# Weight sums by an adding transfer, and the half-wide chunk by seven block products, in the feed-forward nets of a two-layer model

## The chip, the cores and the metric

One Trainium2 chip, one of its cores. The metric is device time of one execution in microseconds, the median of several runs; 1072.19 us before the change (1072.14 to 1073.27 in three runs).

## The reference

Two layers, each with a feed-forward net, a mixer (convolution, recurrence, pooling), cross attention and a second net, with a layer norm behind each. Only the four nets matter here. All is float32, 256 tokens, width 1024, inner width 2816.

```
def swiglu(x, w_gate, w_up, w_down):
    return (jax.nn.silu(x @ w_gate) * (x @ w_up)) @ w_down

h = layer_norm(ALPHA * h + 0.5 * swiglu(h, ffn1_gate[l], ffn1_up[l], ffn1_down[l]), ln_g[l, 0], ln_b[l, 0])
...
h = layer_norm(ALPHA * h + 0.5 * swiglu(h, ffn2_gate[l], ffn2_up[l], ffn2_down[l]), ln_g[l, 3], ln_b[l, 3])
```

## The kernel before

**Numbers.** Each float32 operand is split into a high part (a cast to fp32r by ScalarE, ACT) and a low part (the difference, by VectorE, DVE): `split`, lines 60 to 62. A product is three matmuls: high by high, high by low, low by high (`mm_rows`, line 128). A weight tile of 128 x 1024 numbers (512 KB) is loaded into one of six buffers `raw`, cast to `whi` and differenced to `wlo`, with eight buffers each. So a ninth split waits until the first one's matmuls are done.

**A net.** `ffn` (line 400) goes through the inner width in six chunks: five of 512 columns and one of 256. Up to chunk c's activations it computes x @ gate and x @ up for these columns; then the second half of chunk c - 2's and the first half of chunk c - 1's rows are multiplied by `down` (`both`, line 683). The products of gate and up go to four accumulators `acc`, those of down to four accumulators `dn` that hold the net's whole output. At the end, `tail` adds the last three pieces of `down`, output block by output block, and `finish` (line 303) makes the layer norm and transposes its result for what comes next.

**Three ways to compute a chunk.** `hidden` (line 525) makes 2 x 2 x 8 block products of three matmuls. `by_seven` (line 555) takes x in 2 x 2 blocks (two token blocks, two halves of the width) and gate and up together as 2 x 2 blocks of weights: w00 and w10 are the upper and lower half of gate's rows, w01 and w11 those of up's. Seven block products instead of eight give the four results, from sums and differences of blocks of x (`bx`, made once in a net) and sums of weight blocks. Of the seven products in the kernel before, four have a sum as their weights: w00 + w01, w00 + w11, w01 + w11, w00 + w10. `parts_of` makes each in place with two additions of 128 x 1024 on DVE (line 584), eight in a chunk. `last_hidden` (line 641) computes the half-wide chunk with weights as the stationary operand, so that its results come out transposed, without a deal.

Nets 2 to 4 take chunks 2 and 4 by seven products, the first net chunk 4 alone (line 666). Chunk 5 is the half-wide one, in all nets by `last_hidden`.

**After the products** of the wide chunks the results are combined (`put`, line 605), gated (`left`, line 628), and turned (`turn`, line 446): four transfers deal the gated values `sg` by partitions to `dealt`, DVE transposes them into a buffer `square`, and a split gives the activations `ah` and `al`. The buffers of the half results `half` and of `square` have one tag, "up", with two buffers, so each waits for the one before the last to be done.

**What sets the order.** The code is written in the order of the program; a scheduler then places each engine's instructions in a queue of its own, and each queue runs in order. SP issues nearly all transfers, in order as well; an issue waits until its buffer is free.

Of the kernel before, what the change touches and what calls it, by code (L numbers as in the profile page):

```python
# [8 lines left out]
F32 = mybir.dt.float32  # L9
# [3 lines left out]
ALU = mybir.AluOpType  # L13
# [4 lines left out]
P = 128  # L18
DEPTH = 2
SEQ = 256  # L20
DM = 1024
# [25 lines left out]
def model(ctx: ExitStack, tc: tile.TileContext, t: dict, out: bass.AP):  # L47
# [12 lines left out]
    def split(hi, lo, src):  # L60
        nc.scalar.copy(hi, src)  # L61
        lows.append(nc.vector.tensor_tensor(lo, src, hi.bitcast(F32), op=ALU.subtract))  # L62
# [45 lines left out]
    def sums(o):  # L108
        return o.rearrange("p (c h) -> p h c" if len(o.shape) == 2 else "p r (c h) -> p r h c", h=2)
# [24 lines left out]
    def tok(i):  # L134
        return slice(i * P, (i + 1) * P)
# [264 lines left out]
    def ffn(l, name, n, pend=None, last=False, early=None):  # L400
        gate, up, down = (t[f"{name}_{x}"][l] for x in ("gate", "up", "down"))
        with tc.tile_pool(name="ffn", bufs=2, reuse_waits="tile") as fp:
# [40 lines left out]

            def turn(s):
                ah, al = act_tiles()
                x = fp.tile([P, 4, NT, P], F32, tag="dealt", name="dealt", bufs=1)
                for a in range(4):
                    nc.sync.dma_start(x[a * 32 : a * 32 + 32], s[:, :, a * P : (a + 1) * P])  # L450
                for i in range(NT):
                    d = fp.tile([P, 4, P], F32, tag="up", name="square")
                    nc.vector.transpose(
                        d.rearrange("p k (b r) -> p b k r", b=4), x[:, :, i, :].rearrange("p b (k j) -> p b k j", k=4)
                    )
                    split(ah[:, :, tok(i)], al[:, :, tok(i)], d)
                return ah, al

            def first():
# [62 lines left out]
                        gated(s, i, ou)  # L522
                return turn(s)

            def hidden(c0, between=lambda: None):
                s = activations()
                o = all_products(load(gate, 0, NK, c0, CHUNK))
                for i in range(NT):
                    activate(s, i, o[i])
                between()  # L530
                o = all_products(load(up, 0, NK, c0, CHUNK))
                for i in range(NT):
                    gated(s, i, o[i])
                return turn(s)
# [17 lines left out]
                    split(*parts[n], q[o])  # L552
                return parts

            def by_seven(c0, bx):
                def rows_by_columns(r):
                    return r.rearrange("p (k c) -> p k c", c=CHUNK)

                def pieces(*tags):
                    return [  # L560
                        rows_by_columns(
                            (fp if "spare" in g else wp).tile([P, DM], F32, tag=g, name="raw", bufs=6 if g == "raw" else 1)
                        )
                        for g in tags
                    ]

                def block(m, j, to):
                    for i in range(2):
                        k = 4 * j + 2 * i
                        loads.append(nc.sync.dma_start(  # L570
                            to[i], m[k * P : (k + 2) * P, c0 : c0 + CHUNK].rearrange("(k p) c -> p k c", p=P)
                        ))
                    return to

                w00 = block(gate, 0, pieces("spare0", "spare1"))
                w01 = block(up, 0, pieces("lng", "lnb"))
                w11 = block(up, 1, pieces("raw", "raw"))
                w10 = block(gate, 1, pieces("spare2", "raw"))

                def parts_of(r, plus=None):  # L580
                    hi, lo = [], []
                    for i in range(2):
                        if plus is not None:
                            nc.vector.tensor_tensor(r[i], r[i], plus[i], op=ALU.add)  # L584
                        h = wp.tile([P, 1024], F32R, tag="whi", name="whi", bufs=8)
                        w = wp.tile([P, 1024], F32R, tag="wlo", name="wlo", bufs=8)
                        h, w = (rows_by_columns(x) for x in (h, w))
                        split(h, w, r[i])
                        hi.append(h)
                        lo.append(w)  # L590
                    return Weights(hi, lo, 2, [])

                def part_of_x(i, j):
                    d = slice(4 * j, 4 * j + 4)
                    return xTh[:, d, tok(i)], xTl[:, d, tok(i)]

                def run(o, x, w):
                    for k in range(4):
                        wh, wl = w.at(k, slice(0, CHUNK))
                        mm_rows(o, x[0][:, k, :], x[1][:, k, :], wh, wl, k == 0, k == 3)  # L600

                def half_sum():
                    return fp.tile([P, 4, P], F32, tag="up", name="half").rearrange("p k t -> p (k t)")

                def put(o, a, op, b):
                    nc.vector.tensor_tensor(halves(o), sums(a), halves(b), op=op)

                s = activations()
                g = [s[:, i, :] for i in range(NT)]
                o = [acc((P, CHUNK)) for _ in range(4)]  # L610
# [12 lines left out]
                run(o[0], bx[3], parts_of(w11))  # L623
                run(o[1], part_of_x(0, 1), parts_of(w10))
                run(o[2], part_of_x(1, 1), parts_of(w00, w10))


                def left():
                    put(e, o[0], ALU.add, e)
                    for i in range(NT):  # L630
                        put(g[i], o[1 + i], ALU.add, g[i])
                    s = fp.tile([P, NT, CHUNK], F32, tag="spare2", name="sg", bufs=1)
                    for i, u in enumerate((e, f)):
# [57 lines left out]
            def aside():  # L691

                with tc.issue_after(lows[-1].ins):
                    if bx:
                        rest[1]()
                    else:
                        bx.extend(blocks_of_x())

            for c, (c0, ncol) in enumerate(chunks):
                if not c:  # L700
                    acts.append(first())
                    ys = [[acc((P, 512), "dn") for _ in range(2)] for _ in range(NT)]
                elif c in sevens:
                    left = by_seven(c0, bx)
                else:
                    if c in (1, 2) and early is not None:
                        acts.append(hidden(c0, aside))
                    else:
                        acts.append(hidden(c0) if ncol == CHUNK else last_hidden(c0))
                if c == 1 and early is None:  # L710
                    bx.extend(blocks_of_x())
                if c == max(sevens) + 1:
# [495 lines left out]
```

## Time and profile before

| | |
|---|---|
| profiled execution, its own time | 1072.23 us |
| its span in the profile | 1070.2 us |
| median of three runs | 1072.19 us |
| granted TensorE clock, mean | 0.998 |
| DMA, mean | 217 GB/s |
| second net, from its chunk 2 to its end | 405 to 537 us of the span |

Times in the rows are microseconds from the start of the span, unless marked ns. PE is TensorE, DVE VectorE, ACT ScalarE, POOL GpSimd, SP the engine that issues transfers. In a row in order of time the first number is the start, the second the length of the merged piece (x5: five instructions). Instructions of one engine overlap by the end of their pipeline, so the pitch from one start to the next is shorter than the length of one: a 128 x 512 matmul lasts 0.38 us and the next starts after 0.216. In a row of a group stand its count, then the busy time, the mean ns of one, and the idle time of the engine just before them. A row of a transfer group ends with the KB of one and the median us from issue to landing.

### The profile page before, as it was taken

The numbers are of one execution on the slowest core, as the hardware profiler recorded it, in microseconds if no ns is written. First come the engines' busy times: TensorE is split into PE (matmuls) and PEld (weight loads), VectorE is DVE, ScalarE is ACT, GpSimd is POOL, SyncE is SP. The second block draws the span as 40 slices with busy tenths as digits, with TensorE's granted clock in tenths as the row PEclk, the third lists the DMA queues.
The fourth block names the chain that finished last, engine by engine and source line by source line (L and its number), as shares of the span: only waits on it lengthen the run. The fifth ranks groups of instructions, "written<-read, shape, count | busy, mean of one in ns | idle before, by whom it ended". The sixth has DMA issues, their size and how long they took to land.

```text
span 1070.2 us, 16314 instructions
## 1 busy us (share of the span) xinstructions
PE 1060.6 (99%) x5968; PEld 938.9 (88%) x5968; DVE 946.3 (88%) x1318; ACT 642.2 (60%) x916; POOL 65.0 (6%) x114
## 2 busy tenths in 40 slices
PE   9999999999999999999999999999999999999997
PEld 7888888889899888888888888888898998888886
DVE  6977997998998799999799999788989787999986
ACT  7556655767457565656575557566764665656660
POOL 9600001000000000000000000010000000000000
PEclk9999999999999999999999999999999999999999
DMA  9998395755575575948675875957536665759471
GB/s 360 259 298 269 119 281 167 251 188 159 177 271 168 181 247 198 292 167 226 236 260 192 250 261 173 298 168 227 190 128 208 247 230 176 259 151 341 133 220 40
DMA packets 130896, 231.90 MB, mean 217 GB/s; under 512 B 9409, under 2 KB 48609, under 8 KB 130817
## 3 DMA queue, kind: packets, MB, share of 16 engines
q1 hardware_dynamic: 129024, 228.49, 65.6%
q0 software_dynamic: 1216, 1.20, 0.5%
q8 instruction: 47, 0.77, 0.3%
q10 hardware_dynamic: 576, 1.18, 0.3%
q14 instruction: 33, 0.26, 0.1%
HBM read 216.15 MB, written 1.05 MB: 203 GB/s over the span
## 4 chain that ended last, share of the span: by engine, by line
PE 99%; DMA 0%; DVE 0%; issue 0%; DVEq 0%
PE acc L105 65%; PE dn L105 31%; PE acc L172 1%; PE dn L910 1%; DMA h<-in_x_dram 0%; PE dn L969 0%; PE dn L968 0%; PE dn L958 0%; PE acc L1034 0%; PE dn L472 0%; PE dn L875 0%; DVE h L358 0%; DVE h L353 0%; DVE st L338 0%; DVE h L326 0%
## 5 line engine op out<-in xcount | busy, mean ns | idle before, releaser
L61 ACT CAST whi<-raw 128x1024 fp32r<-128x1024 f32 (+1 forms) x438 | 442.4, 1042 | 199.3 <-DVE raw L584 54.7
L62 DVE TENSOR_TENSOR wlo<-raw,whi 128x1024 fp32r<-128x1024 f32 (+1 forms) x438 | 515.6, 1210 | 33.9 <-ACT whi L61 30.4
L105 PE MATMUL acc<-whi,xT 128*128 128x512 f32 x1032 | 312.9, 380 | 0.0
L105 PEld LDWEIGHTS acc<-whi,xT 128*128 128x128 f32 x1032 | 195.0, 189 | 27.5
L105 PE MATMUL acc<-wlo,xT 128*128 128x512 f32 x516 | 195.6, 379 | 0.0
L105 PE MATMUL acc<-xT,whi 128*128 128x512 f32 x576 | 142.2, 382 | 0.2
L105 PE MATMUL dn<-whi,ah 128*128 128x512 f32 x346 | 131.5, 380 | 0.0
L105 PE MATMUL dn<-wlo,ah 128*128 128x512 f32 x346 | 131.1, 379 | 0.0
L105 PE MATMUL dn<-whi,al 128*128 128x512 f32 x346 | 131.1, 379 | 0.0
L105 PEld LDWEIGHTS acc<-xT,whi 128*128 128x128 f32 x576 | 103.9, 190 | 12.5 <-ACT whi L61 0.7
L105 PEld LDWEIGHTS acc<-wlo,xT 128*128 128x128 f32 x516 | 97.5, 189 | 13.9
L105 PE MATMUL dn<-whi,xT 128*128 128x512 f32 x288 | 87.9, 381 | 0.0
L105 PEld LDWEIGHTS acc<-xT,wlo 128*128 128x128 f32 x576 | 75.5, 191 | 3.9
L105 PE MATMUL acc<-xT,wlo 128*128 128x256 f32 x576 | 75.9, 275 | 0.0
L105 PEld LDWEIGHTS dn<-wlo,ah 128*128 128x128 f32 x346 | 65.4, 189 | 9.2
L105 PEld LDWEIGHTS dn<-whi,al 128*128 128x128 f32 x346 | 65.4, 189 | 9.2
L105 PEld LDWEIGHTS dn<-whi,ah 128*128 128x128 f32 x346 | 65.4, 189 | 9.1
L584 DVE TENSOR_TENSOR raw<-raw 128x1024 f32<-128x1024 f32 x56 | 66.2, 1218 | 0.4
L350 POOL TENSOR_TENSOR rs<-rs,nhalf 128x1 f32<-128x1 f32 x16 | 14.9, 929 | 834.2 <-DVE rs L346 598.7
L105 PEld LDWEIGHTS dn<-whi,xT 128*128 128x128 f32 x288 | 54.6, 190 | 7.4
L105 PE MATMUL dn<-wlo,xT 128*128 128x512 f32 x144 | 54.6, 379 | 0.0
L332 DVE SCALAR_TENSOR_TENSOR h<-h,dn 128x512 f32<-128x512 f32 x31 | 21.2, 683 | 31.6 <-PE dn L105 31.6
(232 smaller groups left out, 1278.7 us busy)
## 6 DMA issues: line engine op xcount, KB each, us to landing
raw<-in_ffn_up_dram SPq DMA_DIRECT2D x88, 512.0 KB, 5.3
raw<-in_ffn_down_dram SPq DMA_DIRECT2D x88, 512.0 KB, 6.9
raw<-in_ffn_gate_dram SPq DMA_DIRECT2D x84, 512.0 KB, 5.0
raw<-in_w_in_dram SPq DMA_DIRECT2D x48, 512.0 KB, 4.7
dealt<-sg SPq DMA_DIRECT2D x80, 128.0 KB, 4.7
raw<-in_ca_k_dram SPq DMA_DIRECT2D x16, 512.0 KB, 5.1
raw<-in_w_out_dram SPq DMA_DIRECT2D x16, 512.0 KB, 4.3
raw<-in_ca_v_dram SPq DMA_DIRECT2D x16, 512.0 KB, 5.3
```

Source lines behind the costliest of these rows:

```text
L61: nc.scalar.copy(hi, src)
L62: lows.append(nc.vector.tensor_tensor(lo, src, hi.bitcast(F32), op=ALU.subtract))
L105: nc.tensor.matmul(o, w, x, start=start, stop=stop)
L172: nc.tensor.transpose(pt[:, k, :], src[:, (4 * j + k) * P : (4 * j + k + 1) * P], unit)
L332: nc.vector.scalar_tensor_tensor(v, v, ALPHA / scale, sums(y[i][n]), op0=ALU.mult, op1=ALU.add, accum_out=None if junk is None else st[:, ...
L350: nc.gpsimd.tensor_tensor(rs, rs, nhalf[:, 0:1], op=ALU.pow)
L584: nc.vector.tensor_tensor(r[i], r[i], plus[i], op=ALU.add)
L910: nc.tensor.matmul(o[g, hh, :], kc[:, hh, g], x, start=True, stop=True)
```

## The change

Four edits, all in `ffn`:

- The first and second block of up are summed by transfers (`sum_by_transfers`): SP loads w01 into the two buffers that else hold the layer norm's parameters, and GpSimd issues a second transfer of w11 with an addition at the destination. This is issued ahead of the up products of the chunk before.
- The seven products are other ones, in another order: first w00, w11 and w10 alone, then S = w00 + w01 + w11, w01 + w11, S - w11 = w00 + w01, and S + w10. With w01 + w11 there already, DVE makes three sums (or differences) of two operations each, six in a wide chunk.
- In nets 2 to 4 the half-wide chunk goes by seven products too, with 256 columns; there DVE also makes the sum w01 + w11. A block is one tile of 4 x 256, so a sum is one addition and a split one pair. The result is dealt and turned like that of a wide chunk.
- `between` holds what stood in `aside`, and issues the transfers.

```
-            sevens = (2, 4) if early is None else (4,)
+            sevens = (2, 4, 5) if early is None else (4,)
...
+            def sum_by_transfers(c0):
+
+                to = block(up, 0, c0, pieces("lng", "lnb"))
+                for i, r in enumerate(to):
+                    a = (4 + 2 * i) * P
+                    nc.gpsimd.dma_start(
+                        r, up[a : a + 2 * P, c0 : c0 + CHUNK].rearrange("(k p) c -> p k c", p=P), accum_op=ALU.add
+                    )
+                return to
...
-                run(o[0], part_of_x(0, 0), parts_of(w00))
-                nc.scalar.copy(halves(g[0]), sums(o[0]))
-                run(o[2], bx[0], parts_of(w00, w01))
-                run(o[1], bx[1], parts_of(w00, w11))
-                e = half_sum()
-                put(e, o[1], ALU.add, g[0])
-                run(o[3], bx[2], parts_of(w01, w11))
-                put(g[1], o[3], ALU.add, e)
-                f = half_sum()
-                put(f, o[2], ALU.subtract, g[1])
-                put(e, o[2], ALU.subtract, e)
-                o = [acc((P, CHUNK)) for _ in range(3)]
-                run(o[0], bx[3], parts_of(w11))
-                run(o[1], part_of_x(0, 1), parts_of(w10))
-                run(o[2], part_of_x(1, 1), parts_of(w00, w10))
+                if ncol < CHUNK:
+                    put(both_up, both_up, ALU.add, w11)
+                o = [acc((P, ncol)) for _ in range(4)]
+                run(o[0], part_of_x(0, 0), parts_of(w00))
+                e = half_sum()
+                nc.scalar.copy(halves(e), sums(o[0]))
+                run(o[1], bx[3], parts_of(w11))
+                f = half_sum()
+                nc.scalar.copy(halves(f), sums(o[1]))
+                run(o[2], part_of_x(0, 1), parts_of(w10))
+                combine(g[0], o[2], ALU.add, e)
+                put(w00, w00, ALU.add, both_up)
+                run(o[3], bx[1], parts_of(w00))
+                combine(e, o[3], ALU.add, e)
+                combine(f, f, ALU.subtract, e, apart=False)
+                o = [acc((P, ncol)) for _ in range(3)]
+                run(o[0], bx[2], parts_of(both_up))
+                combine(g[1], o[0], ALU.add, e)
+                put(both_up, w00, ALU.subtract, w11)
+                run(o[1], bx[0], parts_of(both_up))
+                put(w00, w00, ALU.add, w10)
+                run(o[2], part_of_x(1, 1), parts_of(w00))
...
                 def left():
-                    put(e, o[0], ALU.add, e)
-                    for i in range(NT):
-                        put(g[i], o[1 + i], ALU.add, g[i])
+                    combine(f, o[1], ALU.add, f)
+                    combine(e, o[1], ALU.subtract, g[1])
+                    combine(g[1], o[2], ALU.add, g[1])
...
-                    return turn(s)
+                    return turn(s, ncol // P)
...
+                if c + 1 in sevens:
+                    n = (c + 1) * CHUNK
+                    if n + CHUNK <= DFF:
+                        both_up[:] = sum_by_transfers(n)
...
-                    left = by_seven(c0, bx)
+                    left = by_seven(c0, bx, both_up if ncol == CHUNK else None)
```

Where the queues change. The numbers behind names tell buffers apart. First DVE in the second net, over the last products of chunk 2, before: `square` and `al` are chunk 1's activations, `wlo` low parts of weights, `L584` a weight sum, `half` and `sg` combines; `wlo_4460` belongs to the chunk's last product.

```order
L453 STREAM_TRANSPOSE square_4242<-dealt_4233 128x4x4x32
L62 TENSOR_TENSOR wlo_4434<-raw_4308,whi_4433 128x1024
L62 TENSOR_TENSOR al_4232<-square_4238,ah_4231 128x4x128
L62 TENSOR_TENSOR al_4232<-square_4242,ah_4231 128x4x128
L606 TENSOR_TENSOR half_4382<-acc_4314,sg_4312 128x512
L62 TENSOR_TENSOR wlo_4438<-raw_4309,whi_4437 128x1024
L62 TENSOR_TENSOR wlo_4455<-raw_4296,whi_4454 128x1024
L606 TENSOR_TENSOR sg_4312<-acc_4316,half_4382 128x512
L584 TENSOR_TENSOR raw_4297<-raw_4297,raw_4309 128x1024
L606 TENSOR_TENSOR half_4407<-acc_4315,sg_4312 128x512
L606 TENSOR_TENSOR half_4382<-acc_4315,half_4382 128x512
L62 TENSOR_TENSOR wlo_4460<-raw_4297,whi_4459 128x1024
```

The same place now: `raw` on the left is a weight sum (L596), L622 a combine, and `wlo_4458` and `wlo_4462` belong to the last product.

```order
L596 TENSOR_TENSOR raw_4155<-raw_4304,raw_4308 128x1024
L622 TENSOR_TENSOR sg_4315<-acc_4318,half_4340 128x512
L62 TENSOR_TENSOR wlo_4436<-raw_4154,whi_4435 128x1024
L622 TENSOR_TENSOR half_4340<-acc_4319,half_4340 128x512
L62 TENSOR_TENSOR wlo_4440<-raw_4155,whi_4439 128x1024
L622 TENSOR_TENSOR half_4362<-half_4362,half_4340 128x512
L622 TENSOR_TENSOR sg_4315<-acc_4409,half_4340 128x512
L596 TENSOR_TENSOR raw_4303<-raw_4303,raw_4311 128x1024
L596 TENSOR_TENSOR raw_4304<-raw_4304,raw_4312 128x1024
L622 TENSOR_TENSOR half_4362<-acc_4410,half_4362 128x512
L62 TENSOR_TENSOR wlo_4458<-raw_4303,whi_4457 128x1024
L62 TENSOR_TENSOR wlo_4462<-raw_4304,whi_4461 128x1024
```

The transposes have moved ahead of this piece, and three sums stand between the fifth product's splits and the last one's, where one stood.

Next DVE in the second net's chunk 5, before: the last three of the chunk's four splits of weights (5101 to 5152), then those of the slabs of `down` behind them.

```order
L62 TENSOR_TENSOR wlo_5101<-raw_5093,whi_5100 128x1024
L62 TENSOR_TENSOR wlo_5148<-raw_5143,whi_5147 128x1024
L62 TENSOR_TENSOR wlo_5152<-raw_5144,whi_5151 128x1024
L62 TENSOR_TENSOR wlo_5207<-raw_5202,whi_5206 128x1024
L62 TENSOR_TENSOR wlo_5211<-raw_5203,whi_5210 128x1024
L62 TENSOR_TENSOR wlo_5243<-raw_5238,whi_5242 128x1024
L453 STREAM_TRANSPOSE square_5044<-dealt_5039 128x4x4x32
L453 STREAM_TRANSPOSE square_5048<-dealt_5039 128x4x4x32
L126 TENSOR_TENSOR sg_5090<-acc_5104,sg_5090 128x256
L62 TENSOR_TENSOR al_5038<-square_5044,ah_5037 128x4x128
L62 TENSOR_TENSOR al_5038<-square_5048,ah_5037 128x4x128
```

And now, from the second split of the half-wide chunk on: `square_5047`, `square_5051` and `al_5041` are the activations of chunk 4, `raw_5091` becomes w00 + w01 + w11 and `raw_5093`, which was w01 + w11, becomes w00 + w01.

```order
L62 TENSOR_TENSOR wlo_5124<-raw_5095,whi_5123 128x1024
L62 TENSOR_TENSOR wlo_5142<-raw_5097,whi_5141 128x1024
L596 TENSOR_TENSOR raw_5091<-raw_5091,raw_5093 128x1024
L62 TENSOR_TENSOR wlo_5160<-raw_5091,whi_5159 128x1024
L62 TENSOR_TENSOR wlo_5181<-raw_5093,whi_5180 128x1024
L596 TENSOR_TENSOR raw_5093<-raw_5091,raw_5095 128x1024
L453 STREAM_TRANSPOSE square_5047<-dealt_5042 128x4x4x32
L453 STREAM_TRANSPOSE square_5051<-dealt_5042 128x4x4x32
L62 TENSOR_TENSOR wlo_5199<-raw_5093,whi_5198 128x1024
L62 TENSOR_TENSOR al_5041<-square_5047,ah_5040 128x4x128
L62 TENSOR_TENSOR al_5041<-square_5051,ah_5040 128x4x128
```

Six splits and two sums of chunk 5 stand around the transposes of chunk 4, where four splits stood ahead of them.

Last ACT at that place, now: `ah_5040` are the high parts of chunk 4's activations, `acc_5101` and `acc_5102` the accumulators of the first two products of chunk 5.

```order
L61 CAST whi_5105<-raw_5091 128x1024
L61 CAST whi_5123<-raw_5095 128x1024
L657 ACTIVATE sg_5035<-sg_4834 128x4x4x32
L61 CAST whi_5141<-raw_5097 128x1024
L61 CAST whi_5159<-raw_5091 128x1024
L61 CAST whi_5180<-raw_5093 128x1024
L61 CAST whi_5198<-raw_5093 128x1024
L61 CAST ah_5040<-square_5047 128x4x128
L61 CAST ah_5040<-square_5051 128x4x128
L631 COPY half_5121<-acc_5101 128x256
L634 COPY half_5139<-acc_5102 128x256
```

The copy out of the first accumulator stands behind the casts of chunk 4's activations and six casts of chunk 5's weights; its buffer `half_5121` has the tag "up", as the transposed activations do. On PE the fifth product, of `whi_5180`, goes to the accumulator that this copy frees.

More of the change, by code (lines that the diff above doesn't have):

```diff
@@ L553, in blocks_of_x, with pieces @@
                 return parts
[L555 to L580, printed above, removed]
+            def pieces(*tags, width=CHUNK):
+                return [
+                    (fp if "spare" in g else wp)
+                    .tile([P, DM], F32, tag=g, name="raw", bufs=6 if g == "raw" else 1)
+                    .rearrange("p (k c) -> p k c", c=width)
+                    for g in tags
+                ]
@@ new lines, in by_seven, with put, parts_of @@
+            def by_seven(c0, bx, both_up=None):
+                ncol = min(CHUNK, DFF - c0)
+                if both_up is not None:
+                    w00 = block(gate, 0, c0, pieces("spare0", "spare1"))
+                    w11 = block(up, 1, c0, pieces("raw", "raw"))
+                    w10 = block(gate, 1, c0, pieces("spare2", "raw"))
+                else:
+                    w00, both_up, w11, w10 = (
+                        block(m, j, c0, pieces("raw", width=ncol)) for m, j in ((gate, 0), (up, 0), (up, 1), (gate, 1))
+                    )
+                def put(o, a, op, b):
+                    for x, y, z in zip(o, a, b):
+                        nc.vector.tensor_tensor(x, y, z, op=op)
+                def parts_of(r):
@@ L608, in by_seven, with combine @@
+                def combine(o, a, op, b, apart=True):
+                    nc.vector.tensor_tensor(halves(o), sums(a) if apart else halves(a), halves(b), op=op)
                 s = activations()
-                g = [s[:, i, :] for i in range(NT)]
-                o = [acc((P, CHUNK)) for _ in range(4)]
+                g = [s[:, i, 0:ncol] for i in range(NT)]
+                if ncol < CHUNK:
+                    put(both_up, both_up, ALU.add, w11)
+                o = [acc((P, ncol)) for _ in range(4)]
```

63 lines of the change are left out of this document (33 added, 30 removed).

## The prediction

> **What bounds the kernel now.** I read the page first, for the busy shares and the chain that ended last, and then the nets' stretches by windows and in order of time.
>
> ```profile
> span 1070.2 us, 16314 instructions
> PE 1060.6 (99%) x5968; PEld 938.9 (88%) x5968; DVE 946.3 (88%) x1318; ACT 642.2 (60%) x916; POOL 65.0 (6%) x114
> PE 99%; DMA 0%; DVE 0%; issue 0%; DVEq 0%
> 405.00:537.00 132.00, 132.00 (x633) 116.06 (x632) 121.80 (x140) 77.13 (x92) 0.92 (x1) 1.00 0.68 216
> ```
>
> TensorE (PE) is the whole chain. The last row is a window over the second net from its second chunk to its end; its columns are length, busy PE, weight loads, VectorE (DVE), ScalarE (ACT), GpSimd, granted clock, DMA share, GB/s. PE never waits there, so fewer matmul columns shorten the kernel one for one. But DVE is busy 121.80 of 132 us: PE is only just fed. So each edit has two prices: what it saves PE, and what it does to DVE's lead over PE.
>
> **PE's saving.** The half-wide chunk of the second net:
>
> ```profile
> 505.08 1.67 PE L105 MATMUL acc<-xT,whi 128*128 128x512 f32 x7
> 506.59 1.05 PE L105 MATMUL acc<-xT,wlo 128*128 128x256 f32 x8
> 507.48 1.89 PE L105 MATMUL acc<-xT,whi 128*128 128x512 f32 x8
> ...
> 515.56 0.38 PE L105 MATMUL dn<-whi,ah 128*128 128x512 f32 x1
> ```
>
> Seven 512-wide matmuls start within 1.51 us (0.216 each), eight 256-wide within 0.89 (0.111). The chunk takes 515.56 - 505.08 = 10.48 us. Seven block products of 4 x 3 matmuls of 256 columns are 84 x 0.111 = 9.35 us. Saved: 1.13 us in each of three nets, **3.4 us**. Since PE waits nowhere in the nets, this is all that can be won.
>
> **DVE's prices.** Pitches from runs of equal instructions (the last one's own length taken off):
>
> ```profile
> 440.19 5.76 DVE L62 TENSOR_TENSOR wlo<-raw,whi 128x1024 fp32r<-128x1024 f32 x5
> 447.50 1.30 DVE L453 STREAM_TRANSPOSE square<-dealt 128x512 f32<-128x512 f32 x2
> 448.89 1.29 DVE L62 TENSOR_TENSOR al<-square,ah 128x512 fp32r<-128x512 f32 x2
> 465.85 0.75 DVE L440 TENSOR_TENSOR sg<-acc,sg 128x256 f32<-128x256 f32 x2
> L61 ACT CAST whi<-raw 128x1024 fp32r<-128x1024 f32 x430 | 437.9, 1050 | 199.0 <-DVE raw L584 54.7 <-PE dn L105 50.9 <-PE acc L105 35.8
> L584 DVE TENSOR_TENSOR raw<-raw 128x1024 f32<-128x1024 f32 x56 | 66.2, 1218 | 0.4
> ```
>
> A split's low part is 1.135 us, (5.76 - 1.22) / 4; a weight sum is as long (1218 ns), so 1.135 too; a 512-wide combine, transpose or low part 0.60; a 256-wide one 0.33; ACT's cast 1.05. In a wide chunk 6 sums replace 8: 7 x 2 x 1.135 = 15.9 us less DVE work. In a half-wide one 7 splits replace 4 and 4 sums are new: 3 x 7 x 1.135 = 23.8 us more. The total hardly matters; the place does.
>
> **A, the last product of the first wide chunk (nets 2 to 4).** In the kernel before:
>
> ```profile
> 417.56 5.76 DVE L62 TENSOR_TENSOR wlo<-raw,whi 128x1024 fp32r<-128x1024 f32 x5
> 428.89 0.38 PE L105 MATMUL acc<-wlo,kTh 128*128 128x512 f32 x1
> 432.64 2.36 DVE L62 TENSOR_TENSOR wlo<-raw,whi 128x1024 fp32r<-128x1024 f32 x2
> 434.07 0.38 PE L105 MATMUL acc<-wlo,xT 128*128 128x512 f32 x1
> ```
>
> The fifth product's second low half is made at 423.32 and used at 428.89: a lead of 5.57 us. From there to the seventh product's second half PE needs 24 matmuls, 5.18 us, and DVE 5 x 1.135 + 8 x 0.60 = 10.5 us, so 0.25 should be left; the rows show 433.86 made, 434.07 used. The arithmetic holds, and nothing is left to give. In the changed order the two transposes stand ahead of that point (lead 5.57 - 1.2 = 4.4) and four splits, three sums, two low parts of the activations and five combines behind it: 7 x 1.135 + 7 x 0.60 = 12.15 us. PE waits 12.15 - 5.18 - 4.4 = **2.6 us** (1.1 to 4 with a sum more or less in the lead).
>
> **B, the same place in the other wide chunk.**
>
> ```profile
> 480.91 5.76 DVE L62 TENSOR_TENSOR wlo<-raw,whi 128x1024 fp32r<-128x1024 f32 x5
> 488.46 0.38 PE L105 MATMUL acc<-wlo,kTh 128*128 128x512 f32 x1
> ```
>
> The third of those five is made at 484.40, used at 488.46: lead 4.06. Behind it stand now four sums, four splits and four combines, 8 x 1.135 + 4 x 0.60 = 11.5 us against PE's 5.18. With the old lead the wait is 2.2. Six sums (6.8 us) have left the rows ahead, but eight weight buffers cap the lead near 8 x 1.295 less cast and split, 8 us, which would make it nothing. I take a lead of 5.7, nearer the first end: **0.6 us**, and 0.5 in the first net, which has this chunk alone. DVE then enters the half-wide chunk with no lead.
>
> **C, the fifth block product of the half-wide chunk.** It needs one of four accumulators back, the first product's, which ACT copies out into a buffer of the tag "up". Both that buffer and the copy's place in ACT's queue stand behind the wide chunk's transposed activations.
>
> ```profile
> dealt<-sg SPq DMA_DIRECT2D x80, 128.0 KB, 4.7
> ```
>
> The deal ahead of the transposes (sg to dealt, 4.7 us to landing) lands while DVE still works off splits, and costs nothing beside them. From the last use of that chunk's weights DVE has 10 splits, 3 sums, 3 combines, 2 gatings, 2 transposes and 2 low parts: 13 x 1.135 + 9 x 0.60 = 20.2 us; add 1.1 where a split waits for the cast of a sum just made, and 0.4 for the copy: 21.7. PE meanwhile has 5 + 48 wide matmuls (11.5) and 48 narrow ones (5.3): 16.8. Wait: 4.9, less 0.3 of lead: **4.6 us** (3 to 6).
>
> **E, the rest of that chunk and the tail.** From the copy DVE has four 256-wide combines, a sum and a split until the last product's weights, 3.6 us against PE's 3.2 (25 narrow matmuls and two wide); then six splits and six narrow operations, 8.8 against 8.1. Two waits, 0.4 and 0.7, and the four slab loads are issued only as their buffers come free: **1.4 us** (0.5 to 3).
>
> **D, the net's end (nets 2 and 3).**
>
> ```profile
> 528.71 0.69 DVE L332 SCALAR_TENSOR_TENSOR h<-h,dn 128x512 f32<-128x512 f32 x1 [3.19 <-PE dn L105]
> 532.36 1.41 DVE L358 SCALAR_TENSOR_TENSOR h<-h,rs,lnb 128x512 f32<-128x512 f32 x2
> 533.69 1.04 PE L172 MATMUL acc<-pdn,h 128*128 128x128 f32 x8
> ```
>
> From the first row (h0's sums are complete) to the transposes PE had 24 matmuls, and the norm ends (533.77) as they run. The changed order leaves 20: 0.9 us short. Splits of the next weights now stand between the norm's rows on DVE, and their loads stand behind the new deal on SP's queue, about one split and some landing time, 1.5: **2.4 us** (0.3 to 4).
>
> **The adding transfer.** No row shows one. Below: a plain 512 KB load, 5.3 us. Above: sixteen of POOL's 32 KB pieces one after another, 96 us.
>
> ```profile
> DMA packets 130896, 231.90 MB, mean 217 GB/s; under 512 B 9409, under 2 KB 48609, under 8 KB 130817
> ...
> raw<-in_ffn_up_dram SPq DMA_DIRECT2D x88, 512.0 KB, 5.3
> m<-in_mem_dram POOLq DMA_DIRECT2D x32, 32.0 KB, 6.0
> 429.74 0.37 SPq L570 DMA_DIRECT2D raw<-in_ffn_gate_dram x1
> 461.05 2.48 DVE L584 TENSOR_TENSOR raw<-raw 128x1024 f32<-128x1024 f32 x2
> ```
>
> The nearest row in size is the plain load; I take 7 us. SP issues the block that is added to just ahead of the third row's load, and its first reader is the sum that takes the place of the fourth row's: 31 us, less 5.3 for the load, hide 26 us. So the transfer costs nothing; its 7.3 MB are 3% of the 231.9 MB moved. Nothing but the norm's powers and some clearings waits behind it on POOL; behind its reader on DVE stand all later splits, and PE for them.
>
> **Sum**, on the profiled execution's 1072.23 us (the median of the runs is 1072.19): 3 x (2.6 + 0.6 + 4.6 + 1.4) + 2 x 2.4 + 0.5 - 3.4 = +29.5, **1101.7 us**.
>
> [...] At the start PE runs at half pace:
>
> ```profile
> 5.32 1.63 PE L472 MATMUL dn<-kTh 128*128 128x512 f32 x3
> 7.45 0.78 PE L472 MATMUL dn<-kTh 128*128 128x512 f32 x1
> ```
>
> Three matmuls there take 1.63 us, a pitch of 0.43 against 0.216 later; from 1.53 to about 8.2 us it is so. [...]
>
> **Rivals.**
> 1. *The leads suffice* (the other side). The place is the fifth product of each half-wide chunk. If DVE enters that chunk with 4.6 us of lead, C is gone, and A, B and E shrink the same way; 1072.23 - 3.4 = 1068.8. For it: 2.3 us of sums leave every wide chunk. Against: the 0.2 us left at 434.07, and eight buffers that let no lead be saved up.
> 2. *A and B are hidden*, and C, E and half of D stay: 3 x 6.0 + 2.4 - 3.4 = +17.0, 1089.2. For it: the uncertain leads. Against: A's arithmetic, which the rows above bear out.
> 3. *PE slows after C.* At half pace for up to the start's 6.7 us it loses up to 3.3 us; DVE catches up meanwhile, so E goes: 3 x 1.9 = +5.7, 1107.4. [...]
> 4. *The adding transfer is late.* It decides from 26 us on: at 30 us seven chunks wait 4 us each, 1129.7. Also here: POOL's descriptors were only seen for small pieces.
>
> **How the numbers follow.** Forecast 0.55, rivals 0.07, 0.20, 0.13, 0.05. Rival 1's 0.07 is 0.05 for faster by over 0.2% (2.1 us, about what a measurement of this kernel can tell) and 0.02 for within it, if some waits stay. All else is slower, 0.93. The bounds of the terms together reach from 1083 to 1124; the range leaves out rivals 1 and 4 and the highest sums: 1084 to 1114.
>
> **What would show it.** The half-wide chunk's matmuls as 84 of 256 columns at 0.111; DVE without an idle gap from the fourth wide product on; PE idle before "acc<-whi,kTh" put down to ACT's copy "half<-acc" for some 4 us, three times; smaller waits for casts and low parts at the ends of wide chunks; the adding transfers landed well before a sum of w00. It is wrong if PE's idle time in the nets stays under 3.4 us in all, or if DVE waits for the adding transfer.

## The result and the profile after

The changed kernel takes **1109.19 us** (median of five runs, 1108.13 to 1110.13), the kernel before in the same comparison 1072.19 us. The ratio is 1.0339, with a 95% interval from 1.0324 to 1.0354: 37.0 us slower, where 29.5 were forecast. One run of `pairs`, further down, took 3986.83 us, over three times as long as its others, and is left out of its figures.

The profile's page of the changed kernel, busy shares and the chain that ended last:

```profile
span 1106.2 us, 16547 instructions
PE 1069.9 (97%) x6028; PEld 944.8 (85%) x6028; DVE 958.7 (87%) x1343; ACT 649.4 (59%) x929; POOL 79.6 (7%) x128
PE 82%; DVE 13%; issue 3%; ACT 1%; DMA 1%; SPq 0%; DVEq 0%; ACTq 0%
```

PE was the whole chain before; now 13% of it run through DVE. PE has 60 matmuls more (6028 against 5968): three nets with 84 narrow ones for 64 others. The waits of PE, by what released it (us in total, number of waits, the longest):

```profile
PE acc L105 <- ACT half L631: 12.8, 3, 4.3
PE acc L105 <- DVE wlo L62: 6.3, 7, 1.3
PE acc L172 <- DVE h L358: 4.1, 2, 2.1
PE acc L105 <- ACT whi L61: 3.2, 3, 1.1
```

The first row is the half-wide chunk of three nets (C in the prediction), the third the ends of nets 2 and 3 (D), the second and fourth the ends of the wide chunks (A and B). In order of time, the second net's waits at A and C:

```profile
434.13 0.48 PE L105 MATMUL acc<-whi,xT 128*128 128x512 f32 x1 [1.06 <-ACT whi L61]
435.87 0.48 PE L105 MATMUL acc<-wlo,xT 128*128 128x512 f32 x1 [1.26 <-DVE wlo L62]
519.29 0.38 PE L105 MATMUL acc<-whi,kTh 128*128 128x256 f32 x1 [4.28 <-ACT half L631]
```

Counted from one start to the next, less the usual pitch, these are 1.22, 1.52 and 4.44 us. They are the same in nets 3 and 4 to 0.01 us.

The idle time is not all. Windows of 3.41 us around places A and C (length, then busy time of PE, weight loads, DVE, ACT and GpSimd, each with its number of instructions in brackets, then granted clock, DMA share, GB/s):

```profile
430.79:434.21 3.42, 2.36 (x12) 1.75 (x10) 3.42 (x5) 1.18 (x2) 0.50 (x1) 1.00 0.85 270
434.21:437.62 3.41, 2.15 (x9) 1.67 (x10) 3.41 (x4) 3.41 (x5) 1.86 (x2) 1.00 0.64 160
437.62:441.03 3.41, 3.41 (x18) 2.98 (x17) 3.41 (x6) 3.41 (x4) 0.00 (x0) 1.00 1.12 253
516.13:519.54 3.41, 0.25 (x2) 0.25 (x3) 3.41 (x6) 2.27 (x5) 0.00 (x0) 1.00 0.42 159
519.54:522.95 3.41, 3.41 (x18) 3.41 (x18) 2.96 (x6) 2.70 (x5) 0.00 (x0) 0.50 0.61 202
522.95:526.37 3.42, 3.42 (x27) 3.26 (x27) 3.42 (x5) 3.42 (x4) 0.00 (x0) 1.00 0.71 264
611.71:615.12 3.41, 1.53 (x6) 0.75 (x4) 3.41 (x4) 2.40 (x3) 1.19 (x1) 1.00 0.66 204
615.12:618.53 3.41, 2.97 (x7) 2.41 (x8) 3.41 (x4) 3.41 (x5) 1.20 (x1) 0.50 0.88 210
```

The granted clock is the last number but two. Behind C it is 0.50 for one window (519.54), behind A in net 3 as well (615.12), but not behind the same waits in net 2 (434.21 and 437.62 at 1.00). In the whole run there are six such windows in the nets: behind C in nets 2 and 3, two of them around C in net 4, and behind A in nets 3 and 4. At half pace a full one costs PE half of its 3.41 us, 1.7.

How the 36.1 us of span (1106.2 less 1070.2) build up, from the starts of the same matmuls of `down` in both traces: for each stage, how far it moves the first such matmul behind it.

| stage | predicted | net 1 | net 2 | net 3 | net 4 |
|---|---|---|---|---|---|
| first wide chunk's end (A) | 2.6 | | 2.9 | 4.3 | 4.5 |
| second wide chunk's end (B) | 0.6, net 1 0.5 | 0.6 | 1.2 | 0.9 | 0.9 |
| half-wide chunk (C + E, less 1.13) | 4.9 | | 5.1 | 5.1 | 5.6 |
| net's end (D) | 2.4 | | 2.9 | 2.2 | |

### The profile page after: what moved, and what is told of

It reads as the page before. It is cut to its first block, busy times and chain, and to the rows that moved or that the text cites. A ratio compares the mean times of both kernels' runs of the same rounds, so it can differ in the third digit from the quotient of the medians.

```text
span 1106.2 us, 16547 instructions
## 1 busy us (share of the span) xinstructions
PE 1069.9 (97%) x6028; PEld 944.8 (85%) x6028; DVE 958.7 (87%) x1343; ACT 649.4 (59%) x929; POOL 79.6 (7%) x128
## 4 chain that ended last, share of the span: by engine, by line
PE 82%; DVE 13%; issue 3%; ACT 1%; DMA 1%; SPq 0%; DVEq 0%; ACTq 0%
PE acc L105 52%; PE dn L105 27%; DVE wlo L62 5%; DVE raw L596 3%; PE acc L172 1%; DVE half L622 1%; ACT whi L61 1%; DVE square L453 1%; DVE al L62 1%; DVE sg L622 1%; PE dn L936 1%; DVE h L332 0%; DVE h L358 0%; DMA h<-in_x_dram 0%; PE dn L995 0%
## 5 line engine op out<-in xcount | busy, mean ns | idle before, releaser
L62 DVE TENSOR_TENSOR wlo<-raw,whi 128x1024 fp32r<-128x1024 f32 (+1 forms) x447 | 527.4, 1211 | 63.0 <-ACT whi L61 57.7
L105 PE MATMUL acc<-whi,xT 128*128 128x512 f32 (+1 forms) x1104 | 330.2, 375 | 3.2 <-ACT whi L61 3.2
L105 PEld LDWEIGHTS acc<-whi,xT 128*128 128x128 f32 x1104 | 208.0, 190 | 32.9 <-ACT whi L61 4.4
L105 PE MATMUL acc<-wlo,xT 128*128 128x512 f32 (+1 forms) x552 | 207.6, 376 | 6.3 <-DVE wlo L62 6.3
L105 PE MATMUL acc<-xT,whi 128*128 128x512 f32 x480 | 119.0, 383 | 0.1
L105 PEld LDWEIGHTS acc<-xT,whi 128*128 128x128 f32 x480 | 86.5, 190 | 10.2 <-ACT whi L61 0.4
L105 PE MATMUL acc<-whi,kTh 128*128 128x512 f32 (+1 forms) x160 | 58.5, 366 | 12.8 <-ACT half L631 12.8
L105 PEld LDWEIGHTS acc<-xT,wlo 128*128 128x128 f32 x480 | 62.9, 191 | 3.2
L596 DVE TENSOR_TENSOR raw<-raw 128x1024 f32<-128x1024 f32 x54 | 65.2, 1219 | 0.5
L105 PE MATMUL acc<-xT,wlo 128*128 128x256 f32 x480 | 63.2, 275 | 0.0
L105 PE MATMUL acc<-wlo,kTh 128*128 128x512 f32 (+1 forms) x160 | 58.2, 364 | 0.0
```

The source lines that it names most:

```text
L105: nc.tensor.matmul(o, w, x, start=start, stop=stop)
L596: nc.vector.tensor_tensor(x, y, z, op=op)
```

## Experiments

All times stand against the kernel before on the same chip in the same comparison (1072.12, 1071.77 and 1071.48 us in the three series).

**Which edits cost.** First the half-wide chunk as before:

```
-            sevens = (2, 4, 5) if early is None else (4,)
+            sevens = (2, 4) if early is None else (4,)
```

> The changed kernel, with the half-wide chunk of nets 2 to 4 computed as before. Theory (TensorE waits where VectorE has lost its lead, and the half-rate clock windows that follow are a loss of their own): only the waits at the end of the first wide chunk are left, 2.74 us in each of three nets, with a 1.7 us loss behind those that close the clock, and up to 1.1 us in each of the four second wide chunks: 1072.2 + 8.2 + 1.7 to 5.1 + 1 to 4.4 = 1083 to 1090. Rival 'the half-wide chunk is the whole loss': 1072 to 1074.

1086.75 us, ratio 1.0136 (1.0119 to 1.0153): as the theory had it. The waits at the ends of the wide chunks cost 14.6 us alone, two windows of slow clock behind A included.

Then the other half alone: the wide chunks with the products and sums of before (`by_seven_old`) and without the adding transfer, the half-wide one changed.

```
-                    left = by_seven(c0, bx, both_up if ncol == CHUNK else None)
+                    left = by_seven_old(c0, bx) if ncol == CHUNK else by_seven(c0, bx)
```

> The wide chunks with the seven products, the order and the VectorE sums of the kernel before, no adding transfer; only the half-wide chunk of nets 2 to 4 is the changed one. Theory: no wait at the end of a first wide chunk; VectorE enters the half-wide chunk with two more sums behind it than in the changed kernel, so the wait for the fifth narrow product's accumulator is 4.4 to 6 us, with 1.7 us of slow clock behind each, and the net's ends wait 2.2 us twice: 1072.2 - 3.4 + 3 x (6.1 to 9) + 4.5 = 1091.6 to 1100. Rival 'the loss is in the wide chunks': 1069 to 1074.

1087.38 us, ratio 1.0148 (1.0133 to 1.0163). Its waits of PE:

```profile
PE acc L105 <- ACT half L631: 7.1, 3, 2.5
PE acc L172 <- DVE h L358: 4.1, 2, 2.1
```

No wait at a wide chunk's end, as expected. C is 2.5 us and not the 4.4 to 6 expected: the old order leaves DVE *more* lead at the half-wide chunk, though it makes two sums more. In net 2 DVE starts the first sum of that chunk 6.9 us ahead of PE's first product there (498.17 and 505.05), in the changed kernel 4.3 (rows further down). So the place of the sums counts for more than their number. The two parts make 14.6 + 15.3 = 29.9 of the 37 us; most of the rest is C, which is 1.8 to 2.0 us longer in each of three nets behind the late sums.

**The adding transfer.** Left out, so that w01 + w11 is w01 alone in the wide chunks:

```
-                    nc.gpsimd.dma_start(
-                        r, up[a : a + 2 * P, c0 : c0 + CHUNK].rearrange("(k p) c -> p k c", p=P), accum_op=ALU.add
-                    )
```

> The changed kernel without the adding transfers: w01 + w11 is w01 alone in the wide chunks, so three of seven products there have other weights, and the output is another one. All times of instructions and all other transfers stay. Theory (the adding transfer is hidden and costs nothing): the changed kernel's time within 0.2%, 1107 to 1111.5. Rival 'the adding transfer is late, or its 7.3 MB slow the other loads': at least 3 us less, under 1106.

1107.76 us, ratio 1.0337 (1.0322 to 1.0353), against 1.0339 for the changed kernel: no cost can be told, and the intervals leave room for some 1.6 us. In the changed kernel its row says 8.7 us to landing, where a plain load of that size takes 6.0:

```profile
raw<-in_ffn_up_dram SPq DMA_DIRECT2D x88, 512.0 KB, 6.0
raw<-in_ffn_up_dram POOLq DMA_DIRECT2D x14, 512.0 KB, 8.7
```

**The slow clock behind C.** PE is kept busy where it waits:

```
-                run(o[3], bx[1], parts_of(w00))
+                w = parts_of(w00)
+                for _ in range(4 if ncol < CHUNK else 1):
+                    run(o[3], bx[1], w)
```

> The changed kernel with the fourth narrow product of each half-wide chunk made four times over instead of once (each starts its sum anew, so the values stay): TensorE is given 3 x 12 matmuls of 256 columns, 4.0 us, just where it waits 4.44 us for the accumulator. Theory (the slow windows behind that wait are set off by the idle time): the windows at 0.5 behind the three waits go, four of the six in the profile, about 6.8 us; 1100 to 1105, though TensorE does 12 us more work. Rival 'the windows do not come from the wait' : the same time within 1 us, 1108 to 1110. Rival 'TensorE's work is on the path there': 1113 or more.

1107.93 us, ratio 1.0340 (1.0323 to 1.0356). The windows behind C are gone in all three nets; in net 2:

```profile
516.60:520.14 3.54, 3.28 (x31) 3.09 (x29) 3.54 (x6) 2.46 (x4) 0.00 (x0) 1.00 0.53 154
520.14:523.55 3.41, 3.09 (x25) 2.90 (x25) 3.31 (x7) 2.52 (x4) 0.00 (x0) 1.00 0.61 178
```

So the idle time had closed the clock. But nothing is won in the total. PE, faster behind C, now runs into casts and low parts that aren't ready, in rows that the changed kernel doesn't have:

```profile
PE dn L105 <- ACT whi L61: 1.7, 3, 0.6
PE dn L105 <- DVE wlo L62: 0.7, 3, 0.2
```

These are the waits called E in the prediction. At C the slow clock hides behind DVE, which is late anyway: the half-wide stage of the table gains 0.9 us in the three nets together. In net 2 the run also loses 1.7 us that have nothing to do with C: behind the same waits at A the clock is at 0.50 there (from 435.59 on), where the changed kernel had 1.00. The expected gain of 4 to 9 us failed; that PE does 12 us more work at the half-wide chunks at no cost there shows how far DVE sets the pace.

**The accumulator that C waits for.** Two narrow products share one accumulator, so the fifth has one of its own:

```
+                    t = [acc((P, CHUNK)) for _ in range((n + 1) // 2)]
+                    return [t[i // 2][:, i % 2 * ncol : (i % 2 + 1) * ncol] for i in range(n)]
```

> The changed kernel; in the half-wide chunk two products of 256 columns share one accumulator of 512, so the fifth product has an accumulator of its own and waits for no copy by ScalarE. Rival 'the copy and the accumulator are the cause' (as the prediction put it): the 4.44 us and the slow clock behind them go, three times: 1090 to 1096. Theory after the first four runs (VectorE's work between the two chunks is the cause, the copy only its last link): the fifth product starts some 4 us earlier, the next two then wait for their low parts, and the waits of the chunk sum up to the same 4 to 6 us: 1104 to 1114.

1117.90 us (median of three runs), ratio 1.0430 (1.0411 to 1.0450): slower still. PE in order of time in net 2, then ACT's copies of the first product (L637) and of the second (L640):

```profile
512.77 0.38 PE L105 MATMUL acc<-whi,kTh 128*128 128x256 f32 x1 [0.77 <-ACT whi L61]
514.22 0.38 PE L105 MATMUL acc<-wlo,kTh 128*128 128x256 f32 x1 [1.07 <-DVE wlo L62]
518.96 0.38 PE L105 MATMUL acc<-whi,kTh 128*128 128x256 f32 x1 [3.24 <-ACT half L637]
...
550.69 1.94 PE L172 MATMUL acc<-pdn,h 128*128 128x128 f32 x8 [2.93 <-DVE h L358]
```

```profile
518.53 0.37 ACT L637 COPY half<-acc 128x256 f32<-128x256 f32 x1 [0.91 <-DVE al L62]
521.35 0.37 ACT L640 COPY half<-acc 128x256 f32<-128x256 f32 x1 [1.52 <-PE acc L105]
```

One wait has become three, and the net's end waits longer. But the run does not free PE of the copy. PE makes the first and third product, then the fifth, which waits for its own weights alone (512.77 and 514.22; it is the fifth, since the second of two casts and the second of two low parts made there end these waits). The second and fourth come behind it, from 518.96 on: the second shares the accumulator of the first and waits until that one is copied out (L637), and its own copy (L640) can start only at 521.35. So this run moves the wait for the copy to another product, and does not settle whether the accumulator is the cause; the two runs with early sums below bear on that. The time, above the 1104 to 1114 expected, was not foreseen.

**The place of the sums.** The same seven products in another order in the wide chunks, half-wide chunk as before the change:

```
 run(o[0], part_of_x(0, 0), parts_of(w00))
+put(w00, w00, ALU.add, both_up)
+run(o[1], bx[1], parts_of(w00))
...
+run(o[2], bx[2], parts_of(both_up))
...
+put(both_up, w00, ALU.subtract, w11)
+run(o[3], bx[0], parts_of(both_up))
...
+put(w00, w00, ALU.add, w10)
+run(o[0], part_of_x(1, 1), parts_of(w00))
+run(o[1], bx[3], parts_of(w11))
+run(o[2], part_of_x(0, 1), parts_of(w10))
```

> The changed kernel's wide chunks with the same seven products in another order: the weights that need a sum come second to fifth (S, w01 + w11, S - w11, S + w10), the plain w11 and w10 last; the half-wide chunk as before the change. Adding transfers and the number of VectorE's instructions stay. Theory (the waits at the ends of the wide chunks come from sums that stand where VectorE's lead is already spent): they go, 1071.5 to 1074. Rival 'they come from the adding transfer or from the seven products as such': as with the changed order, 1084 to 1089.

1072.25 us, ratio 1.0008 (0.9999 to 1.0017): the loss falls from 14.6 us in half_by_eight to 0.5. Only the order differs, with what follows from it: ACT copies one accumulator less, and the first product's goes to `sg` and not to a buffer of the tag "up". A and B come from sums behind the point where the lead is spent.

**The lead at the half-wide chunk.** The early sums in all chunks, and chunks 2, 3 and 5 by seven products, so that chunk 4, which goes by eight products and needs no sum, stands ahead of the half-wide one:

```
-            sevens = (2, 4, 5) if early is None else (4,)
+            sevens = (2, 3, 5) if early is None else (4,)
...
```

> All chunks of the change by seven products, with the sums early; the second wide one is chunk 3 instead of 4, so a chunk without sums stands ahead of the half-wide one. Theory (VectorE's lead decides): no wait over 0.5 us in the half-wide chunk and none at the net's end; chunk 3 follows chunk 2 directly and waits 5 to 6 us at its end, with 1.7 us of slow clock: 1072.2 - 3.4 + 3 x 5.6 + up to 3 x 1.7 = 1085 to 1091. Rival 'the half-wide chunk by seven products waits for its accumulator wherever it stands': 4.4 us and more three times beside that, 1098 to 1107.

1098.34 us, ratio 1.0251 (1.0232 to 1.0269). PE's waits in the second net from 500 us on, past the half-wide chunk and the net's end, are this one row:

```profile
PE acc L172 <- DVE h L358: 0.3, 1, 0.3
```

C and E are gone, as the theory said, and D but for 0.3 us; the half-wide chunk gives PE its whole saving, 1.1 us. The fifth product still takes the first one's accumulator, but that is free at once here: with early sums its copy goes to `sg` (L630, 513.32 us), and no longer waits for a buffer of the tag "up". What that alone is worth, early_all below shows. DVE's lead is larger, too: the first sum of the chunk and PE's first product in it stand 4.3 us apart in the changed kernel and 15.2 here:

```profile
505.19 1.22 DVE L596 TENSOR_TENSOR raw<-raw 128x1024 f32<-128x1024 f32 x1
509.49 0.27 PE L105 MATMUL acc<-whi,xT 128*128 128x256 f32 x1
```

```profile
496.19 2.48 DVE L596 TENSOR_TENSOR raw<-raw 128x1024 f32<-128x1024 f32 x2
511.40 0.27 PE L105 MATMUL acc<-whi,xT 128*128 128x256 f32 x1
```

The rival falls with its place, though the total is over the theory's too. In the whole run:

```profile
PE acc L105 <- DVE wlo L62: 14.1, 9, 3.1
```

These are mostly the ends of chunk 3, where two chunks with sums follow each other: 6.1, 6.7 and 4.9 us in the three nets where 5.6 were expected, with shorter waits ahead of it in net 3 and three windows at 0.50 in nets 3 and 4.

**A sum moved to GpSimd.** In that kernel S + w10 of the wide chunks goes to GpSimd:

```
-                        nc.vector.tensor_tensor(x, y, z, op=op)
+                        (nc.gpsimd if b is w10 and len(o) == 2 else nc.vector).tensor_tensor(x, y, z, op=op)
```

> The kernel of early_apart, with the sum S + w10 of the wide chunks, two additions of 128x1024, made by GpSimd instead of VectorE. No run has shown such an addition there; at up to 3 us each it is done before it is needed. Theory: VectorE gets back 2.3 us ahead of the end of chunk 3, the wait there falls from 5.6 to 1 to 3 us, and 1072.2 - 3.4 + 3 x 1 to 3 = 1072 to 1078. Rival 'GpSimd's additions slow VectorE's or come late': over 1082.

1107.81 us, ratio 1.0332 (1.0316 to 1.0348): the rival. DVE and GpSimd at the end of chunk 3 of net 2:

```profile
453.30 1.22 DVE L596 TENSOR_TENSOR raw<-raw 128x1024 f32<-128x1024 f32 x1
...
455.66 2.56 DVE L596 TENSOR_TENSOR raw<-raw 128x1024 f32<-128x1024 f32 x1
458.14 3.44 DVE L62 TENSOR_TENSOR al<-square,ah 128x512 fp32r<-128x512 f32 x2
```

```profile
454.76 2.36 POOL L596 TENSOR_TENSOR raw<-raw 128x1024 f32<-128x1024 f32 x1 [25.85 <-DVE raw L596]
458.38 2.64 POOL L596 TENSOR_TENSOR raw<-raw 128x1024 f32<-128x1024 f32 x1 [1.26 <-DVE raw L596]
```

Where GpSimd adds, DVE's sum takes 2.56 us instead of 1.22, and the two low parts 3.44 instead of 1.29. What DVE is spared it loses in longer instructions: in the whole run it is busy for 968.5 us with 1329 instructions, against 957.8 with 1343 in early_apart. DVE's sum begins at 455.66 inside GpSimd's first addition and ends at 458.22, 1.10 us after that one (457.12), about the time that it takes by itself.

**The slow clock behind A.** The changed kernel once more, and with the first of A's two waits filled:

```
-                run(o[1], bx[0], parts_of(both_up))
+                w = parts_of(both_up)
+                run(o[1], bx[0], w)
+                for k in range(5 if c0 == 2 * CHUNK else 0):
+                    product(o[2], bx[0][0][:, k % 4, :], w.at(k % 4, slice(0, ncol))[0], True, True)
```

> The changed kernel once more, for the two beside it: 1108 to 1110.5.

> The changed kernel; ahead of the last product of chunk 2 TensorE makes five matmuls of 512 columns more (1.08 us) into that product's accumulator, whose sum starts anew behind them, so the values stay. They lie in the first of the two waits there (1.22 us), and only the second (1.52 us) is left idle. Theory (a closed window of 3.41 us follows where about 2 us of one such stretch were idle, and it costs 1.7 us of its own here, since VectorE has its lead back behind this place): no window at 0.5 behind that place in any net, where the changed kernel has them in nets 3 and 4: 2 to 4 us less than the changed kernel beside it. Rival 'as at the half-wide chunk, VectorE is the bound and the slow clock costs little': the same within 1 us.

1107.59 and 1107.92 us, ratios 1.0336 (1.0322 to 1.0350) and 1.0349 (1.0333 to 1.0365): no gain in the total, where the theory expected 2 to 4 us. The traces show both halves of it. Behind A no window is at 0.50, and stage A takes 2.84 us in net 3 and 2.85 in net 4, against 4.53 and 4.43 in the run beside it: 3.3 us less, as expected. But at C in net 3 two windows are now at 0.50 where one was:

```profile
693.00:696.42 3.42, 0.58 (x6) 0.38 (x4) 3.39 (x5) 1.99 (x3) 0.00 (x0) 1.00 0.20 36
696.42:699.83 3.41, 1.98 (x9) 1.98 (x10) 3.32 (x6) 1.56 (x5) 0.00 (x0) 0.50 0.83 272
699.83:703.24 3.41, 3.41 (x18) 3.41 (x18) 2.85 (x4) 3.41 (x5) 0.00 (x0) 0.50 0.55 154
```

The half-wide stage takes 0.9 us more in net 3 and 2.0 more in net 4 (of these, 1.0 is a wait of its own, at 1063.85, whose cause was not followed). So the price of a window behind A is shown, and the saving there was given back at the half-wide chunks.

**All of it with early sums.** The changed kernel's chunks 2, 4 and 5, sums early in all three.

> The changed kernel with the sums early (as in early_sums) in the wide and the half-wide chunk, chunks 2, 4 and 5 by seven products. Theory: nothing is left at the ends of the wide chunks, and the half-wide chunk comes behind a chunk with two sums less on VectorE than in wide_as_before (1087.4), so its waits and the net's ends cost the same or less: 1083 to 1088. Rival 'the changed order matters in the wide chunks alone, the half-wide one costs what it did': 1109.2 less 13 to 15 = 1094 to 1096.

1094.18 us, ratio 1.0212 (1.0198 to 1.0226). The theory expected 1083 to 1088 and failed; the rival's number was met, but not its reason. PE's waits:

```profile
PE acc L172 <- DVE h L358: 5.0, 2, 2.5
PE acc L105 <- ACT whi L61: 2.8, 5, 0.8
PE dn L105 <- DVE wlo L62: 2.8, 6, 1.0
PE acc L105 <- DVE wlo L62: 2.5, 3, 0.8
PE dn L105 <- ACT whi L61: 1.8, 3, 0.7
```

No wait is left at the wide chunks' ends. None is put down to ACT's copy either, but the half-wide chunk has many short ones, and the net's ends wait longer than in the changed kernel. Half-wide chunk and net's end together cost 22.7 us in three nets, against 20.8 there and 15.1 in wide_as_before, by the same marks as in the table. Against early_apart only the place of the second wide chunk differs, and in both the first product's copy goes to `sg`: with 5.3 us between the first sum (499.09) and PE's first product (504.38) the half-wide chunk waits, with 15.2 it does not. So with early sums the lead decides, and freeing the copy is not enough; a buffer of its own for the copy in the changed order was not tried. Why the chunk costs more than in the changed kernel stays open: the order changed in it and in the chunk ahead of it at once. That DVE can't carry a lead past its eight weight buffers is a guess, not tried either.

No version here beats the kernel before. The saving of PE is 3.4 us at most, and every order tried costs more than that or does without the half-wide chunk's seven products.

## Why the prediction was right, and where it was off

- **Direction**, and the size within the range, were right for the reason given: PE had no idle time, DVE just kept up, and the change moved DVE's work behind the places where its lead is spent. early_sums shows it at the wide chunks, early_apart beside early_all at the half-wide one.
- **PE's saving**: the first four narrow products, 48 matmuls, run from 509.49 us to 4.44 us ahead of 519.29, 5.36 us: 0.112 each, as predicted.
- **A**, predicted at 2.6 us, is 2.74 of idle time. **The step that failed is here**: the sum put the slow clock behind A at nothing; the prediction weighed it behind C alone, in rival 3. Behind A in nets 3 and 4 the clock did close, 1.7 us each, and the stage took 4.3 and 4.5. This is the largest part of what the sum lacked: 3.9 of 6.6 us between the forecast's 29.5 and the span's 36.1, as the first row of the table shows.
- **B**, predicted at 0.6 (0.5 in the first net), is 0.76 to 1.11 us of idle time (0.51): by the same sum the lead there was 5.2 to 5.6 us where 5.7 were taken. The stages are 1.3 us over in all.
- **C**, predicted at 4.6, is 4.44, released by ACT's copy as written. early_all and early_apart add that a free copy is not enough and that DVE's lead decides, both with early sums; pairs does not settle it.
- **E**, predicted at 1.4, is not in the changed kernel. Rival 3 came true beside the forecast in the place it named: PE at half pace behind C, DVE catching up, E gone. That half pace follows such a wait was the author's estimate: before's trace has the clock at 1.00 from 8.26 to 1066.39 us. Its window costs 1.7 us (more in net 4, with two), and E costs about 1.1 where the clock stays up (fill_c), so the stage is 0.2 to 0.7 us over. That the forecast for the stage held is therefore luck in part: a term that it had is not there, and one that it left out is there at about the same size. The rival's other number, half pace for 6.7 us, was too long in nets 2 and 3: one window of 3.41. Its total, 1107.4, is nearer to the result than the forecast's 1101.7, but by luck too: it put 1.9 us more a net at C, where 0.2 to 0.7 are measured, and nothing at A, where most of the difference lies.
- **D**, predicted at 2.4, is 2.23 of idle time, and this agreement is luck. The prediction left PE four matmuls less in that time, 20, and let DVE make one split more. From the first row below to the transposes PE has 25 matmuls, two more than before (23, and not 24), and three splits stand between the norm's rows, not one:

```profile
540.44 0.69 DVE L332 SCALAR_TENSOR_TENSOR h<-h,dn 128x512 f32<-128x512 f32 x1 [2.84 <-PE dn L105]
...
541.05 1.22 DVE L62 TENSOR_TENSOR wlo<-raw,whi 128x1024 fp32r<-128x1024 f32 x1
...
542.79 1.22 DVE L62 TENSOR_TENSOR wlo<-raw,whi 128x1024 fp32r<-128x1024 f32 x1
...
544.66 1.22 DVE L62 TENSOR_TENSOR wlo<-raw,whi 128x1024 fp32r<-128x1024 f32 x1
...
547.18 1.41 DVE L358 SCALAR_TENSOR_TENSOR h<-h,rs,lnb 128x512 f32<-128x512 f32 x2
```

  From the first row to the last it takes 6.74 us, against 3.65 before: 3 x 1.135 for the splits and 1.2 for two more rows of L332 between them, less a gap of 1.31 that DVE had there for ACT and 0.2 of small rows. Nothing of it is landing time.
- **The adding transfer** is hidden, as predicted, and took 8.7 us where 7 were assumed. Rival 4 is out, and so are rivals 1 and 2, whose leads were not there.

## What to carry to other kernels

Where one engine is just fed by another, price an edit by what it puts behind the point where the feeder's lead is smallest, not by the work that it saves: six sums instead of eight cost 14.6 us here, and the same six in another order none that can be told. A wait that one semaphore ends may have a whole queue behind it; and an edit that is to free one resource can make another instruction wait for it, so read in the trace who waits now. And short waits of TensorE can cost more than their length: the two at A, 1.22 and 1.52 us, cost 1.7 us more in slow clock in nets 3 and 4 here, and none in net 2.

## What was unexpected of the hardware

**Half pace came behind waits of 1.22 and 1.52 us.** The six windows at 0.50 in the changed kernel's nets start a multiple of 3.413 us apart (615.12 - 519.54 = 28 x 3.413, and two in net 4 follow each other at 1069.09 and 1072.50). In the 3.41 us ahead of each, PE was busy for 0.25 to 1.53 us; the 1.53 (611.71, above) hold two waits of 1.22 and 1.52 us and none longer. In net 2 the same two waits lie in two stretches with 2.36 and 2.15 us of busy PE (430.79 and 434.21, above), and the clock behind both was 1.00. In half_by_eight they left a stretch of net 3 with 1.80 us, and the clock behind it was 1.00 too:

```profile
606.37:609.78 3.41, 1.80 (x7) 1.38 (x8) 3.41 (x5) 3.41 (x5) 2.38 (x2) 1.00 0.65 181
609.78:613.19 3.41, 3.41 (x18) 2.99 (x17) 3.41 (x5) 3.41 (x5) 0.00 (x0) 1.00 1.06 221
```

In nets 2 and 4 of that run 1.10 us of busy PE (432.29 and 968.19) were followed by 0.50.

**DVE's additions took longer beside GpSimd's.** 128 x 1024 numbers take GpSimd 2.83 us on average (14 additions in gpsimd_sum; 2.36 and 2.64 in the rows above), and meanwhile DVE's sum of 1.22 took 2.56. DVE's 40 sums there average 1.52 us, against 1.22 for the 54 in early_apart.

**The adding transfer is cheap**: 8.7 us for 512 KB, against 6.0 for a plain load in the same run, and no change of the time that could be told (no_adding).
